# A two-layer mLSTM and retention backbone: mLSTM parts in another order, norm products at fixed positions in the last step of a stage, first two units of a stage by segment

## The chip, the cores and the metric

The kernel runs on one core of one Trainium2 chip. The metric is the device time of one execution in microseconds; what is compared is the median over runs. Engines are named as in the profile: PE is TensorE (matmuls), PEld its weight loads, DVE is VectorE, ACT ScalarE, POOL GpSimd, SP SyncE.

## The reference, cut to what matters

512 tokens of 1024 channels go through two layers. 256 of them are context tokens (segment 0), 256 latent ones (segment 1). Each layer is a half SwiGLU feed-forward, a token mixer and another half feed-forward; each of these six stages begins with an RMSNorm with a per-segment shift and scale. The mixer of the first layer is a bidirectional mLSTM, that of the second a retention.

```
def rmsnorm(h, g):
    y = hf * lax.rsqrt(jnp.mean(hf * hf, axis=-1, keepdims=True) + NORM_EPS)
def modnorm(h, g, mod, j):
    return rmsnorm(h, g) * (1 + mod[:, :, 3 * j + 1]) + mod[:, :, 3 * j]
def half_ffn(h, mod, g, w13, w2, j):
    return h + FFN_RES * mod[:, :, 3 * j + 2] * swiglu(modnorm(h, g, mod, j), w13, w2)

# one chunk of 128 tokens of the mLSTM, for one direction
s = jnp.einsum("bhtd,bhsd->bhts", q, k) * jnp.exp(d - m_t[..., None])
num = w_inter[..., None] * jnp.einsum("bhtd,bhde->bhte", q, C) + jnp.einsum("bhts,bhse->bhte", s, v)
den = w_inter * jnp.einsum("bhtd,bhd->bht", q, n) + jnp.sum(s, axis=-1)
h = num / jnp.maximum(jnp.abs(den), jnp.exp(-m_t))[..., None]
C = w_prev[..., None, None] * C + jnp.einsum("bhs,bhsd,bhse->bhde", w_s, k, v)
```

## The kernel before, in words

The residual stream XT, and the normed input as a high and a low half (xh, xl), lie channel-major in SBUF. Every weight arrives by DMA from SP as raw, and is split into wh (ACT, L148) and wl (DVE, L149). Every product is three matmuls, mm3 at L152 to L154: high by high, low by high, high by low. PSUM has four A banks and four Y banks. The six stages run in the order f00, mlstm, f01, f10, retention, f11; each is a list of units, and most units bring one weight slice of 256 columns. The matmul's moving side is 512 tokens wide, or 256 where a segment is handled by itself. Where the code has no in_order() block, a scheduler sets each engine's order from a model of the times, with the order of the code as its priority; within in_order() PE's order is that of the code.

A norm goes so. As soon as a channel tile of XT is final, ACT squares it (L170) and POOL adds the squares up into nacc (L174); the tiles 0, 6 and 7 keep theirs apart. L179 sums over channels with PE. L159 (DVE) and L161 (POOL) make rsa and rsb, the reciprocal root. L186 spreads it over the partitions with PE. Then DVE and ACT apply it tile by tile, L196 to L203: even tiles take three instructions, t, xh and xl; odd tiles go through split2 (L148, L149). In the last step of a stage (fn1 of the feed-forward, and of wout in mlstm) the products of segment 0 come first, then those of segment 1 (L414 and L594), so that segment 0's norm runs beside them; segment 1's norm comes after, beside the first products of the next stage.

mlstm at 8 heads: qk(0) to qk(3) make the queries and keys, each followed by a convolution on DVE; vo(0) and vo(1) the values of the two halves of heads, vo(2) and vo(3) the output gates; gates makes the decays, from which come nwd (in DRAM), em, ws and wp. For half hh: ktok transposes the keys (L710), states makes the chunk states C (L732), intra(s, hh) the outputs of segment s, fin(s, hh) the head norm, the gating and the transposes; wout(hh, u) projects half hh onto 512 of the output channels.

intra is the tightest part. L754 makes the scores, in two A banks. For each direction d a tile b4 (two buffers) is read from nwd by a DMA of POOL (L762), masked on POOL (L769), run through eight exps on ACT (L772) and multiplied with the scores on DVE (L775, twice). For each chunk c PE multiplies it with the values (L786) and adds the queries by C (L791), into two A banks; ACT and DVE make dn (L795 to L797), and hs from it (L801 on ACT for d = 0, L803 on DVE for d = 1). The scores hold their banks until L775 of the second direction. fin takes statistics (L817, L818), the reciprocal root as above, nb (L821), scales (DVE L824, ACT L827), gates on POOL (L832) and transposes with PE (L835) into xh and xl.

Of the kernel before, what the change touches and what calls it, by code (L numbers as in the profile page):

```python
# [23 lines left out]
KT = 8  # L24
# [64 lines left out]
def build(nc, tc, dr, out):  # L89
# [42 lines left out]
    sv = ExitStack()  # L132
# [69 lines left out]
                S.activation(out=h, in_=t, func=AF.Identity, bias=b_)  # L202
                V.scalar_tensor_tensor(out=lo, in0=t, scalar=b_, in1=h.bitcast(F32), op0=ALU.add, op1=ALU.subtract)  # L203

    def norm_seg(N, s, l, j):
        ps = bankA() if s == 0 else bankY()
        norm_apply(s, l, j, norm_bcast(norm_rstd(N, s, ps), ps))

    def accum(k, ps, gate, s):

# [65 lines left out]
    def ffn(l, which, segs, groups, on_tile, on_seg, first="seg"):  # L276
# [27 lines left out]
        for d0, nd in parts:  # L304
            for p in range(d0, d0 + nd, 2):
                sv = {}
                for ab in range(2):
                    col = ab * DFF + p * 128
                    src = w13[:, col:col + 256].rearrange("(k p) c -> p k c", p=128)

                    def half(W, hf, p=p, ab=ab, sv=sv):
                        if hf == 0:
                            sv["ps", ab] = {m: bankY() if first == "k" and p == 2 and ab == 0 else bankA() for m in range(2)}
                        ps = sv["ps", ab]
                        cols = [(a, z)]
                        if p == 0 and first == "seg" and len(segs) > 1:
                            cols = [(s * 256, s * 256 + 256) for s in segs]
                        for b, e in cols:
                            for h in (range(2) if len(cols) > 1 else (hf,)):
                                ks = range(h * 4, h * 4 + 4)  # L320
                                order = [(k, m) for k in ks for m in range(2)] if p == 0 else [
                                    (k, m) for m in range(2) for k in ks]
                                for k, m in order:
                                    mm3(ps[m][:, b:e], [W(i, k)[:, m * 128:(m + 1) * 128] for i in range(2)],
                                        (xh[:, k, b:e], xl[:, k, b:e]), k == 0, k == KT - 1)
                                if h == 0 and e == z:
                                    W.mid()

                    def done(p=p, ab=ab, sv=sv):
                        ps = sv["ps", ab]  # L330
                        for m in range(2):
                            if ab == 0:
                                sv[m] = P["s"].tile([128, 512], F32, name="s", tag="s")
                                S.activation(out=sv[m][:, a:z], in_=ps[m][:, a:z], func=AF.Silu)
                            else:
                                g = P["s"].tile([128, 512], F32, name="s", tag="s")
                                V.tensor_tensor(out=g[:, a:z], in0=sv[m][:, a:z], in1=ps[m][:, a:z], op=ALU.mult)  # L337
                                gh = P["g"].tile([128, 512], F32R, name="gh", tag="gh")
                                gl = P["g"].tile([128, 512], F32R, name="gl", tag="gl")
                                split2(g[:, a:z], gh[:, a:z], gl[:, a:z])  # L340
                                gs[p + m] = (gh, gl)

                    def fn(W, half=half, done=done, by_seg=p == 0 and first == "seg" and len(segs) > 1):
                        half(W, 0)
                        if not by_seg:
                            half(W, 1)
                        done()

                    if first == "k" and p == 0:
                        def fn0(W, ab=ab, sv=sv):  # L350
                            sv["ps", ab] = U["ps", ab] = {m: bankA() for m in range(2)}
                            first_products[ab](W)
                        res.append((fn0, src, "own"))
                        late.append((lambda W, done=done: done(), None, None))
                        if ab:
                            res += [(start, None, None)] + late
                    else:
                        res.append((fn, src, "kn" if p == 0 and first == "seg" else "k" + narrow))
            ku = [(k, min(4, d0 + nd - k)) for k in range(d0, d0 + nd, 4)]
            fin = d0 == parts[-1][0]  # L360
            for mg in range(2):
                Y = {}
                for k0, nk in ku:
# [6 lines left out]
                    last = k0 == ku[-1][0]  # L370
                    stop = last or (pair and k0 == ku[-3][0])

                    def products(W, Y, b, e, k0, nk, first, stop, done, Wm=None):
                        for h0 in range(0, nk, 2):
                            for m in range(4):
                                for k in range(h0, h0 + 2):
                                    i = mm3(Y[m][:, b:e], [W(i, k)[:, m * 128:(m + 1) * 128] for i in range(2)],
                                            [x[:, b:e] for x in gs[k0 + k]], first and k == 0, stop and k == nk - 1)
                                if stop and h0 + 2 == nk:
                                    done(m)  # L380
                            if h0 == 0 and Wm:
                                Wm.mid()
                        return i
# [19 lines left out]
                    def fn1(W, k0=k0, nk=nk, Y=Y):  # L403
# [5 lines left out]
                                on_tile(s, 4 + m)  # L409
                            return fn  # L410
                        i = products(W, Y, 0, 256, k0, nk, False, True, done(0))
                        on_seg(0)
                        Y.update({m: bankY() for m in range(4)})
                        with tc.issue_after(i.ins):  # L414
                            products(W0, Y, 256, 512, k00, nk0, True, False, None)
                            W.mid()
                            products(W, Y, 256, 512, k0, nk, False, True, done(1))
                        on_seg(1)
# [45 lines left out]
    def mlstm(on_tile, on_seg):  # L464
# [29 lines left out]
        def qk(u):  # L494
            src = win[:, u * 256:(u + 1) * 256].rearrange("(k p) c -> p k c", p=128)

            def fn(W):
                pp = {m: bankA() for m in range(2)}
                for b, e in ([(0, 256), (256, 512)] if u == 0 else [(0, 512)]):
                    for hf in range(2):  # L500
                        ks = range(hf * 4, hf * 4 + 4)
                        for k, m in ([(k, m) for k in ks for m in range(2)] if u == 0 else
                                     [(k, m) for m in range(2) for k in ks]):
                            mm3(pp[m][:, b:e], [W(i, k)[:, m * 128:(m + 1) * 128] for i in range(2)],
                                (xh[:, k, b:e], xl[:, k, b:e]), k == 0, k == KT - 1)
                        if hf == 0 and e == 512:
                            W.mid()
                for m in range(2):
                    c = u * 2 + m
                    pad = t2k(n=520).rearrange("p (s t) -> p s t", s=2)  # L510
# [7 lines left out]
                        V.scalar_tensor_tensor(out=cs, in0=pad[:, :, w:w + 256], scalar=CW[:, w * 8 + c:w * 8 + c + 1],  # L518
                                               in1=cs, op0=ALU.mult, op1=ALU.add)
                    S.activation(out=X["q" if c < 4 else "k"][c % 4 // 2][:, c % 2, :], in_=cv, func=AF.Silu)  # L520
            return (fn, src, "kn" if u == 0 else "k")

        def vo(u):
            Y = {}
# [34 lines left out]
        def wout(hh, u):  # L559
            src = dr["m_out"][hh * 512:(hh + 1) * 512, u * 512:(u + 1) * 512].rearrange("(k p) c -> p k c", p=128)  # L560

            def products(W, Y, u, b, e, done, Wm=None):
                for h0 in (0, 2):
                    for m in range(4):
                        for k in (h0, h0 + 1):
                            kk = hh * 4 + k
                            i = mm3(Y[m][:, b:e], [W(i, k)[:, m * 128:(m + 1) * 128] for i in range(2)],
                                    [z[:, kk, b:e] for z in ((xh, xl) if hh else X["y"])], k == 0, k == 3)
                        if h0:
                            done(u, m, Y[m])  # L570
                    if h0 == 0 and Wm:
                        Wm.mid()
                return i
# [16 lines left out]
            def fn1(W):  # L590
                W0 = X["W"]
                i = products(W, {m: bankA() for m in range(4)}, 1, 0, 256, done((0,)))
                on_seg(0)
                with tc.issue_after(i.ins):  # L594
                    products(W0, {m: bankY() for m in range(4)}, 0, 256, 512, done((1,)))
                    W.mid()
                    products(W, {m: bankY() for m in range(4)}, 1, 256, 512, done((1,)))
                on_seg(1)
# [2 lines left out]
        def part(f, *a):  # L601
            return (lambda W: f(X, *a), None, None)

        res += [qk(0), part(gates), qk(2)] + vo(0) + [qk(1), qk(3)]
        v1, v2, v3 = vo(1), vo(2), vo(3)

        res += [part(ktok, 0), part(states, 0), part(intra, 0, 0)] + v1 + [part(intra, 1, 0)]
        res += v2[:1] + [part(ktok, 1)] + v2[1:] + [part(states, 1), part(fin, 0, 0), part(fin, 1, 0)]
        res += v3[:1] + [part(intra, 0, 1)] + v3[1:] + [wout(0, 0), part(intra, 1, 1), wout(0, 1)]
        res += [part(fin, 0, 1), part(fin, 1, 1), wout(1, 0), wout(1, 1)]  # L610
        res.append((lambda W: st.close(), None, None))
        return res

# [625 lines left out]
                nc.sync.dma_start(out=out[t * 128:(t + 1) * 128, h * 512:(h + 1) * 512], in_=o[h])  # L1239

    def into(N, l, j):
        return (lambda s, k: norm_tile(N, s, k)), (lambda s: norm_seg(N, s, l, j))

    both = (0, 1)
    f00 = ffn(0, 0, both, [(0, range(4, 6)), (0, range(6, 10)), (0, range(10, 16))], *into(N1, 0, 1), first="k")
# [86 lines left out]
```

## Time and profile before

| | us |
|---|---|
| median of three runs (lowest, highest) | 1880.07 (1878.45, 1880.35) |
| the profiled execution: its time | 1882.0 |
| its span, first to last instruction | 1880.0 |
| PE busy | 1841.9 (98%) |
| DVE, ACT, POOL busy | 1189.4, 697.1, 166.6 |
| mean granted clock of PE | 0.992 |

A busy PE is one in which a matmul is under way; as matmuls overlap, the spacing of their starts tells more than their durations. Two ends are read from a wait: where it stood, and what its first matmul no longer overlaps with. PEclk is the granted clock of a stretch: 1.00 is the 2.4 GHz level, 0.50 the 1.2 GHz one.

### The profile page before, as it was taken

The numbers are of one execution on the slowest core, as the hardware profiler recorded it, in microseconds if no ns is written. First come the engines' busy times: TensorE is split into PE (matmuls) and PEld (weight loads), VectorE is DVE, ScalarE is ACT, GpSimd is POOL, SyncE is SP. The second block draws the span as 40 slices with busy tenths as digits, with TensorE's granted clock in tenths as the row PEclk, the third lists the DMA queues.
The fourth block names the chain that finished last, engine by engine and source line by source line (L and its number), as shares of the span: only waits on it lengthen the run. The fifth ranks groups of instructions, "written<-read, shape, count | busy, mean of one in ns | idle before, by whom it ended". The sixth has DMA issues, their size and how long they took to land.

```text
span 1880.0 us, 25438 instructions
## 1 busy us (share of the span) xinstructions
PE 1841.9 (98%) x10142; PEld 1594.1 (85%) x10142; DVE 1189.4 (63%) x1966; ACT 697.1 (37%) x1061; POOL 166.6 (9%) x204
## 2 busy tenths in 40 slices
PE   8999999999999799999999999999999999999998
PEld 6888888887788788888889888888898888889998
DVE  6858877565968566777755655555466555575554
ACT  4432233243564443223233432232254444444443
POOL 2000000110233200000001000000112120110001
PEclk9999999999999899999999999999999999989999
DMA  8545655322433234555552335545324244335652
GB/s 317 184 141 197 207 189 191 110 92 76 128 106 125 101 113 135 167 193 177 177 182 90 124 123 185 207 157 181 110 101 140 95 135 135 103 122 177 205 180 90
DMA packets 171832, 280.58 MB, mean 149 GB/s; under 512 B 6353, under 2 KB 108881, under 8 KB 171329
## 3 DMA queue, kind: packets, MB, share of 16 engines
q1 hardware_dynamic: 168800, 268.59, 42.3%
q0 software_dynamic: 2912, 10.36, 1.8%
q8 instruction: 80, 1.31, 0.3%
q14 instruction: 38, 0.31, 0.0%
q10 hardware_dynamic: 2, 0.01, 0.0%
HBM read 277.82 MB, written 1.11 MB: 148 GB/s over the span
## 4 chain that ended last, share of the span: by engine, by line
PE 90%; DVE 5%; ACT 2%; issue 1%; POOL 0%; DMA 0%; SPq 0%; POOLq 0%; DVEq 0%; ACTq 0%
PE A L153 18%; PE A L154 18%; PE A L152 18%; PE Y L153 11%; PE Y L152 11%; PE Y L154 11%; DVE wl L149 1%; PE A L786 1%; ACT wh L148 1%; PE Y L1094 1%; DVE XT L211 0%; PE Y L179 0%; DVE t L201 0%; DVE mj L1098 0%; ACT x L1109 0%
## 5 line engine op out<-in xcount | busy, mean ns | idle before, releaser
L149 DVE TENSOR_TENSOR wl<-raw,wh 128x1024 fp32r<-128x1024 f32 x360 | 448.7, 1247 | 465.4 <-ACT wh L148 465.1
L148 ACT ACTIVATE wh<-raw 128x1024 fp32r<-128x1024 f32 x360 | 382.9, 1064 | 784.1 <-PE A L153 321.8
L153 PE MATMUL A<-xl,wh 128*128 128x512 f32 (+1 forms) x1712 | 598.1, 351 | 7.0 <-DVE xl L149 6.2
L152 PE MATMUL A<-xh,wh 128*128 128x512 f32 (+1 forms) x1712 | 592.1, 352 | 4.6 <-ACT xh L1111 2.6
L154 PE MATMUL A<-xh,wl 128*128 128x512 f32 (+1 forms) x1712 | 596.6, 350 | 0.0
L153 PEld LDWEIGHTS A<-xl,wh 128*128 128x128 f32 x1712 | 324.1, 189 | 51.4 <-DVE xl L149 7.3
L152 PEld LDWEIGHTS A<-xh,wh 128*128 128x128 f32 x1712 | 320.3, 190 | 47.7 <-ACT xh L1111 2.9
L154 PEld LDWEIGHTS A<-xh,wl 128*128 128x128 f32 x1712 | 324.1, 189 | 42.2
L248 DVE CUSTOM_DVE_ANT_0 mj<-mr,mc,VB 128x1024 bf16<-128x1024 f32 x224 | 287.0, 1281 | 3.9 <-DMA mr<-mod_t 1.1
L154 PE MATMUL Y<-gh,wl 128*128 128x512 f32 (+1 forms) x704 | 244.2, 347 | 0.0
L153 PE MATMUL Y<-gl,wh 128*128 128x512 f32 (+1 forms) x704 | 244.0, 347 | 0.0
L152 PE MATMUL Y<-gh,wh 128*128 128x512 f32 (+1 forms) x704 | 243.6, 347 | 0.0
L154 PEld LDWEIGHTS Y<-gh,wl 128*128 128x128 f32 x704 | 132.2, 188 | 16.8
L153 PEld LDWEIGHTS Y<-gl,wh 128*128 128x128 f32 x704 | 132.1, 188 | 16.7
L152 PEld LDWEIGHTS Y<-gh,wh 128*128 128x128 f32 x704 | 132.0, 188 | 16.8
L153 PE MATMUL Y<-wl,xh 128*128 128x512 f32 x320 | 126.1, 394 | 0.0
L154 PE MATMUL Y<-wh,xl 128*128 128x512 f32 x320 | 125.6, 393 | 0.0
L152 PE MATMUL Y<-wh,xh 128*128 128x512 f32 x320 | 125.5, 394 | 0.0
L174 POOL TENSOR_TENSOR nacc<-nacc,nsq 128x256 f32<-128x256 f32 x50 | 41.3, 836 | 643.9 <-ACT nsq L170 642.8
L148 ACT ACTIVATE gh<-s 128x512 fp32r<-128x512 f32 (+1 forms) x88 | 48.9, 570 | 84.0 <-DVE s L337 83.9
L211 DVE SCALAR_TENSOR_TENSOR XT<-Y,GT,XT 128x256 f32<-128x256 f32 x148 | 63.7, 479 | 18.7 <-PE Y L154 18.5
L337 DVE TENSOR_TENSOR s<-s,A 128x512 f32<-128x512 f32 (+1 forms) x88 | 54.3, 619 | 27.7 <-PE A L154 26.2
(272 smaller groups left out, 1771.2 us busy)
## 6 DMA issues: line engine op xcount, KB each, us to landing
raw<-w SPq DMA_DIRECT2D x126, 1024.0 KB, 5.0
mr<-mod_t SPq DMA_DIRECT2D x128, 512.0 KB, 3.8
raw<-r_in SPq DMA_DIRECT2D x24, 1024.0 KB, 5.0
raw<-m_in SPq DMA_DIRECT2D x12, 1024.0 KB, 5.1
raw<-r_out SPq DMA_DIRECT2D x8, 1024.0 KB, 6.1
raw<-w SPq DMA_DIRECT2D x12, 512.0 KB, 3.7
w<-mod_t SPq DMA_DIRECT2D x8, 512.0 KB, 9.7
w<-mod_s SPq DMA_DIRECT2D x8, 512.0 KB, 10.1
```

The lines of the kernel that those rows point to most:

```text
L148: S.activation(out=hi, in_=src, func=AF.Copy)
L149: return V.tensor_tensor(out=lo, in0=src, in1=hi.bitcast(F32), op=ALU.subtract)
L152: TE.matmul(ps, l[0], r[0], start=first, stop=False)
L153: TE.matmul(ps, l[0], r[1], start=False, stop=False)
L154: return TE.matmul(ps, l[1], r[0], start=False, stop=last)
L174: G.tensor_tensor(out=N[s][0], in0=N[s][0], in1=sq, op=ALU.add)
L211: V.scalar_tensor_tensor(out=XT[:, k, seg(s)], in0=ps, scalar=gate[:, s, k:k + 1], in1=XT[:, k, seg(s)], op0=ALU.mult, op1=ALU.add)
L248: V.tensor_tensor_reduce(out=mp["j"], in0=raw[i], in1=mp["c"][:, w], scale=1.0, scalar=MB[:, l * 72 + f:l * 72 + f + 1], op0=ALU.mult, op1 ...
L337: V.tensor_tensor(out=g[:, a:z], in0=sv[m][:, a:z], in1=ps[m][:, a:z], op=ALU.mult)
L786: TE.matmul(pb[g][:, i, :], E[:, i * 4 + g * 2 + c], v[:, s * 2 + c, 2 * i + g, :], start=(i == 0 or n == 0), stop=(n == 0))
L1094: TE.matmul(ps, U["w", k][:, 0, c * 128:(c + 1) * 128], SC.rearrange("p (w k) -> p k w", w=2)[:, c], start=(c == 0), stop=(c == KT - 1))
```

## The change

Three things are changed.

The norm of segment 0 in the last step of f00, mlstm, f01 and f10: norm_seg with steps gives back two pieces of work, and the loop over segment 1's products calls the first (sums) ahead of its fifth product and the second (broadcast and application) ahead of its tenth. A product is three matmuls. The loop is now in_order().

The first two units of mlstm (qk(0), qk(2)) and of f01 and f10 (their first two slices) do segment 0 of both, then segment 1 of both; qk(2) had done 512 tokens at once.

The list of mlstm's parts has another order.

```
-        norm_apply(s, l, j, norm_bcast(norm_rstd(N, s, ps), ps))
+        def sums():
+            r.append(norm_rstd(N, s, ps))
+        def rest():
+            norm_apply(s, l, j, norm_bcast(r[0], ps))
+        if steps:
+            return {4: sums, 9: rest}
...
                 i = products(W, {m: bankA() for m in range(4)}, 1, 0, 256, done((0,)))
-                on_seg(0)
-                with tc.issue_after(i.ins):
-                    products(W0, {m: bankY() for m in range(4)}, 0, 256, 512, done((1,)))
+                norm = on_seg(0, True)
+                with tc.issue_after(i.ins), in_order():
+                    products(W0, {m: bankY() for m in range(4)}, 0, 256, 512, done((1,)), among=norm)
...
+                if u == 0:
+                    X["first"] = W, pp
+                    products(W, pp, 0, 256, True)
+                elif u == 2:
+                    W0, pp0 = X["first"]
+                    products(W, pp, 0, 256, False)
+                    products(W0, pp0, 256, 512, False)
+                    W.mid()
+                    conv(0, pp0)
+                    products(W, pp, 256, 512, False)
+                    conv(2, pp)
...
-        res += [qk(0), part(gates), qk(2)] + vo(0) + [qk(1), qk(3)]
+        res += [qk(0), qk(2), part(gates)] + vo(0) + [qk(1), qk(3)]
...
-        res += [part(ktok, 0), part(states, 0), part(intra, 0, 0)] + v1 + [part(intra, 1, 0)]
-        res += v2[:1] + [part(ktok, 1)] + v2[1:] + [part(states, 1), part(fin, 0, 0), part(fin, 1, 0)]
-        res += v3[:1] + [part(intra, 0, 1)] + v3[1:] + [wout(0, 0), part(intra, 1, 1), wout(0, 1)]
-        res += [part(fin, 0, 1), part(fin, 1, 1), wout(1, 0), wout(1, 1)]
+        res += [part(ktok, 0), part(states, 0), part(intra, 0, 0)] + v2[:1] + [part(intra, 1, 0)] + v2[1:]
+        res += [part(fin, 0, 0), part(fin, 1, 0), part(ktok, 1)] + v1 + [part(states, 1), part(intra, 0, 1)]
+        res += v3[:1] + [part(intra, 1, 1)] + v3[1:] + [part(fin, 0, 1), wout(0, 0), part(fin, 1, 1), wout(0, 1)]
+        res += [wout(1, 0), wout(1, 1)]
```

Line numbers behind L179 shift in the changed kernel: L754, L786, L791 and L835 of before are L801, L833, L838 and L882 after.

The end of mlstm on PE, before: the last direction of intra(1,1) (L786, L791) and the transposes of fin (L835). The products Y<-yh,wh are those of wout(0,1), the products A<-xh,wh those of wout(1,0).

```order
L154 MATMUL Y<-yh,wl 128x512
L786 MATMUL A<-v_3922,b_4928 128x129 x4
L791 MATMUL A<-C_4391,t 128x129 x4
L786 MATMUL A<-v_3922,b_4928 128x129 x4
L791 MATMUL A<-C_4367,t 128x129 x4
L152 MATMUL Y<-yh,wh 128x512
L153 MATMUL Y<-yl,wh 128x512
L154 MATMUL Y<-yh,wl 128x512
L835 MATMUL A<-ident,hs 128x128 x16
L152 MATMUL A<-xh,wh 128x256
```

Of the products of wout(0,1), 15 stand ahead of this direction and 3 behind it.

The same place on PE, after: from the scores of intra(1,1) (L801) to wout(1,0).

```order
L801 MATMUL A<-qk_3048 128x128 x8
L833 MATMUL A<-v_4368,b_4774 128x129 x4
L838 MATMUL A<-C_4504,t 128x129 x4
L833 MATMUL A<-v_4368,b_4774 128x129 x4
L838 MATMUL A<-C_4528,t 128x129 x4
L833 MATMUL A<-v_4368,b_4843 128x129 x4
L838 MATMUL A<-C_4540,t 128x129 x4
L833 MATMUL A<-v_4368,b_4843 128x129 x4
L838 MATMUL A<-C_4516,t 128x129 x4
L882 MATMUL A<-ident,hs 128x128 x16
L152 MATMUL A<-xh,wh 128x256
```

All products of wout(0,0) and wout(0,1) now stand ahead of these rows, and both directions follow the scores directly.

The last step of f00 on PE, before: where the broadcast of segment 0's norm stands. The sums (L179) come after 26 matmuls of segment 1, this after 60 in all.

```order
L152 MATMUL Y<-gh,wh 128x256
L153 MATMUL Y<-gl,wh 128x256
L154 MATMUL Y<-gh,wl 128x256
L186 MATMUL A<-ident,rsb 128x128 x2
L152 MATMUL Y<-gh,wh 128x256
L153 MATMUL Y<-gl,wh 128x256
```

The same step after: the sums, with the first twelve matmuls of segment 1 ahead of them.

```order
L153 MATMUL Y<-gl,wh 128x256
L154 MATMUL Y<-gh,wl 128x256
L179 MATMUL A<-ones,nacc 128x1 x6
L152 MATMUL Y<-gh,wh 128x256
L153 MATMUL Y<-gl,wh 128x256
```

The broadcast follows 15 matmuls behind the sums.

## Rows read from the trace of the kernel before

**Rows 1.** The page: busy us of each engine (share of the span), instructions.

```profile
PE 1841.9 (98%) x10142; PEld 1594.1 (85%) x10142; DVE 1189.4 (63%) x1966; ACT 697.1 (37%) x1061; POOL 166.6 (9%) x204
```

**Rows 2.** Waits of PE over the span: total us, times, longest us.

```profile
PE A L835 <- POOL hs L832: 9.4, 1, 9.4
PE A L153 <- DVE xl L149: 6.2, 6, 1.7
```

**Rows 3.** Border f00 to mlstm: timeline (start, us, what, [idle before]); window (us, PE busy, ...).

```profile
396.33 1.39 PE L179 MATMUL A<-ones,nacc 128*128 128x1 f32 x12
398.65 0.72 POOL L161 TENSOR_TENSOR rsb<-rsa,mhalf 128x2 f32<-128x2 f32 x1 [4.66 <-DVE rsa L159]
401.68 0.60 PE L186 MATMUL A<-ident,rsb 128*128 128x128 f32 x4
409.13 0.39 PE L153 MATMUL A<-xl,wh 128*128 128x256 f32 x1 [1.66 <-DVE xl L149]
414.54 0.60 PE L186 MATMUL Y<-ident,rsb 128*128 128x128 f32 x4
...
406.00:431.00 25.00, 21.79 (x148) 1.00 0.35 110
```

**Rows 4.** End of mlstm: timeline of PE; windows (us, PE busy, PEclk, DMA share, GB/s).

```profile
617.31 0.72 PE L791 MATMUL A<-C,t 64*128 64x129 f32 x8
629.24 2.34 PE L835 MATMUL A<-ident,hs 128*128 128x128 f32 x8 [9.45 <-POOL hs L832]
631.23 0.56 PE L152 MATMUL A<-xh,wh 128*128 128x256 f32 x1
...
618.00:631.30 13.30, 3.74 (x22) 0.73 0.23 79
624.00:634.40 10.40, 5.05 (x23) 0.51 0.46 157
631.60:634.30 2.70, 2.70 (x14) 0.50 0.85 329
```

**Rows 5.** Windows of 256-column, 512-column, and 512-column weight-moving products.

```profile
386.05:392.05 6.00, 6.00 (x53) 1.00 0.54 175
209.00:256.00 47.00, 47.00 (x209) 1.00 0.53 173
424.00:431.00 7.00, 7.00 (x32) 1.00 0.39 117
```

**Rows 6.** Longest wait of PE at the borders after mlstm, f01 and f10: timeline.

```profile
659.98 0.39 PE L153 MATMUL A<-xl,wh 128*128 128x256 f32 x1 [0.63 <-DVE xl L149]
1025.98 0.39 PE L153 MATMUL A<-xl,wh 128*128 128x256 f32 x1 [1.56 <-DVE xl L149]
1391.69 0.39 PE L153 MATMUL A<-xl,wh 128*128 128x256 f32 x1 [1.59 <-DVE xl L149]
```

**Rows 7.** Weights of intra(0,0): the second eight exps, and their first use: timeline.

```profile
483.55 2.46 ACT L772 ACTIVATE b<-b,a 128x128 f32<-128x128 f32 x8
514.26 0.61 PE L786 MATMUL A<-v,b 128*128 128x129 f32 x4
```

**Rows 8.** Weights of intra(1,1), and the freeing of a bank: timeline; median landing, us.

```profile
590.42 0.58 POOL L762 DMA_DIRECT2D b<-nwd  x1 [1.99 <-PE A L786]
596.27 1.69 POOL L769 TENSOR_SCALAR_AFFINE_SELECT b<-b 128x1024 f32<-128x1024 f32 x1 [5.26 <-DMA b<-nwd]
597.99 2.47 ACT L772 ACTIVATE b<-b,a 128x128 f32<-128x128 f32 x8 [2.87 <-POOL b L769]
602.81 2.49 DVE L775 SCALAR_TENSOR_TENSOR b<-A,b 128x512 f32<-128x512 f32 x4
610.00 1.15 ACT L801 ACTIVATE hs<-A,dn 128x128 f32<-128x128 f32 x4 [0.37 <-DVE dn L797]
...
b<-nwd POOLq DMA_DIRECT2D x8, 512.0 KB, 4.7
```

## What the change will do to the time: the prediction

> **What bounds the kernel now.** I read the page's summary first: PE is busy for 1841.9 of 1880.0 us [rows 1]. So nearly every microsecond that a change can give lies in stretches where PE stands still or runs at the lower clock. The waits of PE say where these are. The longest single wait is 9.4 us, L835 (the transposes of the last mLSTM heads) for the gated heads of L832; then come six waits of 6.2 us in all, the longest 1.7, for the low half xl (the odd tiles, L149) [rows 2]. The six are boundaries between stages: the first products of the next stage wait until the RMSNorm of a segment has been summed (L179), rooted (L159, L161), broadcast (L186) and applied.
>
> Two stretches were then read instruction by instruction. At the border f00 to mLSTM [rows 3] the sums of segment 0 start at 396.33, 26 matmuls after the first segment-1 product, rsb follows on GpSimd at 398.65, and the broadcast stands on PE only at 401.68. PE runs out of work at 407.5 and idles 1.66 us for xl. Segment 1 follows with four shorter waits. Of 25.00 us between 406 and 431, 21.79 are busy, so 3.2 are idle [rows 3]. A first matmul after a wait also loses its overlap: it is 0.39 us long where its successors come every 0.118, so I count 5 x 0.27 = 1.4 more: 4.6 us lost at this border.
>
> At the end of mLSTM [rows 4] the last intra matmuls (L791) end at 618.0. Then dn, the last hs on DVE, the head norm's statistics, its reciprocal root on GpSimd, scaling and gating lie one behind the other; the transposes resume at 629.24 after 9.45 us of idle, and wout(1,0) starts at 631.23. From 624.00 to 634.40 the granted clock is 0.51, that is, the 1.2 GHz level, and the products of wout(1,0) come every 0.21 us in it (2.70 us for 12 to 13) rather than every 0.118: some 15 of them, about 1.5 us, and a further 1.2 on the transposes. The tail costs about 9.5 + 2.7 = 12 us.
>
> **The change part by part.** The arithmetic is the same. Only qk(2) has more matmuls: 96 of 256 columns for 48 of 512. At 6.00/51 = 0.118 us and 47.00/207 = 0.227 us [rows 5] (two of each window's count were under way at its start), that is 11.3 for 10.9, or **+0.4 us**.
>
> *Norms at fixed positions, first two units by segment.* At f00 to mLSTM the sums come after 12 matmuls rather than 26 and the broadcast 15 matmuls (1.8 us) later; the last squares that they need may come some tenths after PE gets there. The chain of segment 0 then starts at about 394.7, 1.6 us sooner, and its broadcast, which had stood 5.4 us behind the sums, stands about 3 behind: it comes some 4 us sooner. That covers the 1.66. After the broadcast of segment 1, 16 matmuls of segment 0 are left (1.9 us); from L186 at 414.54 PE goes on until its waits at about 416 to 418, so that 0.7 to 1.2 us remain. **Gain 3.5 us.** On the three later borders the longest idle was 0.63, 1.56 and 1.59 us [rows 6]. In the new order 9 products follow the second broadcast at f01 (1.1 us, about what is lost there now: no gain), 21 at f10 (2.5 us, which covers most: gain 1.5), and at retention the broadcast stands only 4 matmuls behind the sums, so PE may wait there for rsa and rsb: gain 1.7, give back 0.5. **Sum of the later borders: 2.7, bounds 0.5 to 4.**
>
> *The order of the mLSTM parts.* The gates are computed 11 us later, since the 96 products of qk(2) now stand ahead of them; from their results come the exps of intra(0,0)'s weights, the second set of which ACT ends at 486.0, for a first use by PE at 514.26 [rows 7]; 11 us later they still arrive in time, and the cover is vo(0), qk(1) and qk(3). The products of wout(0,0) and wout(0,1), 96 matmuls, are what fills the tail today: the order of before has 43 + 29 + 1 + 15 + 3 of them between intra(0,1) and the last transposes. In the new one fin(0,0) and fin(1,0) come sooner, so these products are free sooner, and the order spends all 96 between the states of the second half and the end of intra(0,1): 4 are left ahead of the scores of intra(1,1), and from there to wout(1,0) there is none, as the quoted rows show.
>
> So PE meets the tail with nothing to do, and the tail becomes a chain of latencies. From the first mLSTM product at 406.4 to there the new order has 596 matmuls of 512 columns (0.227 or, with the weight as the moving side, 7.00/30 = 0.233 us apart [rows 5]: 136.5 in all), 192 of 256 (22.7) and some 200 small ones, 37 us by the starts of their like in the trace (0.18 on average): 196. With 2 us of remaining stalls PE ends intra(0,1) at about 604.5. That frees the second weight buffer (b4 has two). From there [rows 8] give: issue 0.5 on GpSimd; from issue to landing 4.7, the median of the eight, though one took 5.8 (590.42 to 596.27); the select 1.4 (this one 1.69); eight exps 2.5; two products on DVE at 0.62 each and half a microsecond of what stands between them, 1.7: 604.5 + 0.5 + 4.7 + 1.4 + 2.5 + 1.7 = 615.3. Only then can the second chunk of direction 0 run, because the banks that it needs hold the scores which direction 1 reads. Second chunk of direction 0, first of direction 1, bank freed through dn and hs (1.8: hs alone is 1.15 on ACT), second chunk: 1.8 + 1.8 + 1.8, so 620.7 (a pair of L786 and L791 groups is 1.8 by the pair that ends at 618.03). From the last L791 to the resumed transposes are 11.2 us today (618.0 to 629.24) and to wout(1,0) 13.2: **634.0 for 631.23, a loss of 2.8 us**, in which the 3.5 of the first border and the 0.4 of qk(2) are contained. With 5.8 us of landing it is 635.1, with as much less 632.9, and if the first buffer is late too, 636.
>
> *The clock in it.* In the present tail PE is busy for 3.74 of 13.30 us, at a mean granted clock of 0.73 [rows 4]. In the new one it has about 9 us of work in the 30 from 604.5 to 634, the same share, so I take the same 0.73 for the small matmuls there: 9/0.73 is 3.3 more, of which about half stand on the chain just added up (the first scores and the first chunk run while something else is waited for). I take **1.5**, bounds 0 and 3.3. The recovery in wout(1,0) costs what it costs now.
>
> The Trainium skill (page "DMA: Bandwidth & Descriptors", section "Anatomy of one DMA") has a GpSimd-issued copy at about 2 us fixed plus bytes over 436 GB/s, 3.2 us for these 512 KB: an estimate by that page that would bring the tail 1.5 us forward and the time to about 1880. The trace has 4.7 as its median, 1.5 more than that fit, and the sum goes by the trace.
>
> **Sum.** 1882.0 (the profiled execution, 1880.0 span and 2.0 around it) + 2.8 + 1.5 - 2.7 = 1883.6. The median of the runs is 1.9 below the profiled execution, so about 1881.7; I say **1882**. That lies within 0.2% of 1880.07 (3.8 us, about what a measurement of this kernel can tell from no change).
>
> **Rivals.** (a) *The tail is covered after all.* If the first wait of 9.4 goes because the heads of fin(0,1) and fin(1,1) end while PE still has products, the 9.5 and the 2.7 of clock are saved, with 3.5 at the border, 0.4 of qk(2) against and 2.7 later: 1880 - 18 = 1862. Even half of the wait gives 1870. For it speaks that both fin parts stand earlier in the text; against it, that no filler is left in the row of PE. It decides itself by whether the new chain ends before 629. (b) *Slower, by the weight buffers.* If both copies of the b4 tiles of intra(1,1) take the longer landing, and the small matmuls all run at the 1.2 GHz level, the tail ends at 636, the clock costs 3.3 on the intra matmuls and another 1.5 on wout(1,0), if as many of its products again run at 0.21: +4.8 + 4.8 - 2.7 = +6.9, 1887; with the later borders giving only 0.5, 1889. The point from which it decides is a wout(1,0) that starts later than about 636. (c) *The fixed positions wait themselves.* With PE's order fixed, a sums product whose squares are late, or a broadcast 15 matmuls (1.8 us) behind the sums whereas rsb ends 1.65 us behind them today (397.72 to 399.37) and rsa can stand behind the split of a weight on DVE, stops PE at each of four borders for 0.5 to 1.5 us: the borders give nothing and the time is 1884 to 1886.
>
> **How the numbers follow.** The forecast, between 1876.3 and 1883.8, gets 0.42. (a), whole or in part, gets 0.25: the reading of the order is firm, but the chain has ten steps, and two microseconds less in it with the borders at their best is enough for 1876. (b) and (c) get 0.33 together. The range reaches to half of (a), 1869, and to the end of (b) with a little over, 1890.
>
> **What would show it.** Right: the idle ahead of the transposes is split into several waits from about 605 to 633, wout(1,0) starts at 632.5 to 636 on the present time line, the 1.66 at the first border is gone, and the 1.56 and 1.59 too. The 1.2 GHz level would hold for longer than the present 10.4 us. Wrong: a tail in which wout(1,0) starts before 629, wout(0,1) products still running on PE when the last intra ends, or new waits of L186 for rsb at the borders that eat the gain.

## The result and the profile after

The changed kernel takes 1891.97 us (median of 4 runs, 1888.17 to 1894.37) where before takes 1880.06; the ratio is 1.0063, 95% interval 1.005 to 1.0075. It is slower by 0.63%, and 2 us above the upper end of the forecast range.

The page and the waits of PE of the changed kernel (total us, times, longest us):

```profile
PE 1848.2 (98%) x10190; PEld 1602.7 (85%) x10190; DVE 1188.6 (63%) x1966; ACT 698.3 (37%) x1063; POOL 168.3 (9%) x204
PE A L882 <- POOL hs L879: 10.7, 3, 8.4
PE A L833 <- DVE hs L850: 4.7, 1, 4.7
...
PE A L152 <- ACT xh L202: 2.2, 2, 1.1
PE A L801 <- DVE hs L850: 2.0, 1, 2.0
PE Y L186 <- POOL rsb L161: 1.6, 2, 1.0
PE A L179 <- POOL nacc L174: 1.4, 1, 1.4
PE A L833 <- ACT hs L848: 1.2, 1, 1.2
```

Against [rows 2], the six waits for xl have left the list. In their place stand waits inside intra (L801, L833), two more ahead of the transposes, and one of the sums L179 for nacc. Windows of the changed kernel (us, PE busy, PEclk, DMA share, GB/s), the border f00 to mlstm first, then the stretches at the 1.2 GHz level that matter:

```profile
406.00:431.00 25.00, 25.00 (x207) 1.00 0.25 69
611.00:622.00 11.00, 5.39 (x36) 0.69 0.41 139
631.90:642.10 10.20, 4.45 (x20) 0.50 0.21 72
655.80:662.60 6.80, 6.80 (x33) 0.50 0.01 4
1410.00:1413.60 3.60, 3.60 (x19) 0.53 0.00 0
```

The border that idled for 3.2 us [rows 3] is busy throughout: all its idle is gone. Where the time went is told by the same landmarks in each trace. Executions differ by up to 2 us in when f00 ends, so I measure between landmarks (line numbers shift by a few in the runs): S0, S1, S2 and S3 are the first product of segment 1 in the last step of f00, mlstm, f01 and f10; W is the start of wout(1,0); G is the one pair of gates products that spreads the maxima over the partitions (L677, after: L724), nearly the last thing that gates asks of PE; I is the first weighted product of intra(0,0) (L786, after: L833); R is the first sums product of the norm behind retention. In the changed kernel's timeline of PE (start, us, what, [idle before]) S0, G, I, the waits in the tail and W are:

```profile
391.52 0.28 PE L152 MATMUL Y<-gh,wh 128*128 128x256 f32 x1
477.76 0.48 PE L724 MATMUL A<-rows,ones 1*128 1x128 f32 x2
524.21 0.68 PE L833 MATMUL A<-v,b 128*128 128x129 f32 x4
611.84 0.90 PE L801 MATMUL A<-qk 64*128 64x128 f32 x4 [1.99 <-DVE hs L850]
618.20 1.20 PE L833 MATMUL A<-v,b 128*128 128x129 f32 x4 [4.71 <-DVE hs L850]
626.22 1.01 PE L833 MATMUL A<-v,b 128*128 128x129 f32 x6 [1.20 <-ACT hs L848]
637.54 0.69 PE L882 MATMUL A<-ident,hs 128*128 128x128 f32 x2 [8.36 <-POOL hs L879]
639.53 0.56 PE L152 MATMUL A<-xh,wh 128*128 128x256 f32 x1
```

and in that of before S0 and G, beside W and I of [rows 4, 7]:

```profile
393.27 0.28 PE L152 MATMUL Y<-gh,wh 128*128 128x256 f32 x1
468.85 0.48 PE L677 MATMUL A<-rows,ones 1*128 1x128 f32 x2
```

The same differences for every kernel of this study, in us (S0 to G is 477.76 less 391.52 in the changed one, and so on). Each row is one profiled execution, the medians are of all; kernels with the same order of PE differ by up to 1.6 us in a stretch (G to I is 46.7 in f4, 45.1 in h1), so a difference below that in one row can be one of executions:

| kernel | S0-G | G-I | I-W | S0-W | W-S1 | S1-S2 | S2-S3 | S3-R | median us |
|---|---|---|---|---|---|---|---|---|---|
| before | 75.6 | 45.4 | 117.0 | 238.0 | 12.8 | 365.7 | 366.2 | 298.0 | 1880.1 |
| changed | 86.2 | 46.4 | 115.3 | 248.0 | 12.6 | 369.8 | 364.3 | 299.4 | 1892.0 |
| e1_norm | 75.2 | 45.4 | 116.8 | 237.3 | 13.2 | 365.1 | 364.3 | 299.3 | 1879.8 |
| e2_first_two | 84.0 | 44.6 | 116.9 | 245.5 | 12.6 | 365.9 | 366.2 | 298.8 | 1888.5 |
| e3_parts | 75.6 | 45.4 | 116.3 | 237.3 | 13.4 | 365.7 | 366.2 | 298.6 | 1878.9 |
| e4_no_parts | 86.2 | 45.5 | 110.9 | 242.7 | 12.1 | 370.4 | 364.3 | 299.4 | 1886.8 |
| f1_gates_late | 83.6 | 45.9 | 112.3 | 241.8 | 12.1 | 365.7 | 366.2 | 298.8 | 1884.7 |
| f2_gates_early | 73.7 | 45.2 | 114.6 | 233.4 | 13.3 | 369.1 | 364.3 | 300.2 | 1881.4 |
| f3_no_step_mlstm | 86.2 | 46.2 | 115.6 | 248.0 | 13.4 | 365.9 | 364.3 | 300.2 | 1889.1 |
| f4_gates_early_two | 73.7 | 46.7 | 114.1 | 234.6 | 12.5 | 366.8 | 364.3 | 298.6 | 1876.8 |
| g6_hold | 86.2 | 46.2 | 113.3 | 245.7 | 12.0 | 369.9 | 364.3 | 299.6 | 1891.2 |
| g4_short_weights | 86.2 | 41.9 | 110.1 | 238.3 | 12.7 | 368.2 | 364.3 | 298.8 | 1875.9 |
| g5_f4_old_list | 73.7 | 46.6 | 117.7 | 238.0 | 13.3 | 365.7 | 364.3 | 298.1 | 1878.6 |
| h1_gate_dve | 73.7 | 45.1 | 113.3 | 232.1 | 12.4 | 365.6 | 364.3 | 298.2 | 1874.0 |

So the changed kernel loses 10.0 us from S0 to W and 4.1 from S1 to S2, gains 1.9 from S2 to S3, and loses 1.4 from S3 to R; behind R it gains 0.8. The loss up to W is about as large as the delay of the gates, 10.6.

### The profile page after: what moved, and what is told of

It reads as the page before. It is cut to its first block, busy times and chain, and to the rows that moved or that the text cites. A ratio compares the mean times of both kernels' runs of the same rounds, so it can differ in the third digit from the quotient of the medians.

```text
span 1890.9 us, 25521 instructions
## 1 busy us (share of the span) xinstructions
PE 1848.2 (98%) x10190; PEld 1602.7 (85%) x10190; DVE 1188.6 (63%) x1966; ACT 698.3 (37%) x1063; POOL 168.3 (9%) x204
## 3 DMA queue, kind: packets, MB, share of 16 engines
HBM read 277.82 MB, written 1.11 MB: 148 GB/s over the span
## 4 chain that ended last, share of the span: by engine, by line
PE 91%; DVE 2%; ACT 2%; DMA 1%; issue 1%; POOL 1%; POOLq 0%; DVEq 0%; SPq 0%; ACTq 0%
PE A L153 18%; PE A L152 18%; PE A L154 18%; PE Y L152 11%; PE Y L153 11%; PE Y L154 11%; PE Y L1141 1%; PE A L833 1%; ACT b L819 0%; DMA mc<-cc 0%; ACT wh L148 0%; DMA t<-nwd 0%; PE Y L179 0%; PE A L179 0%; POOL nacc L174 0%
## 5 line engine op out<-in xcount | busy, mean ns | idle before, releaser
L341 ACT ACTIVATE s<-A 128x512 f32<-128x512 f32 (+1 forms) x86 | 46.1, 536 | 69.7 <-PE A L154 69.7
```

## The experiments

Ratios are to the kernel before on the same chip, with 95% intervals. The first four take the change apart.

**e1_norm**: the fixed norm positions alone.

```
-                on_seg(0)
-                with tc.issue_after(i.ins):
+                norm = on_seg(0, True)
+                with tc.issue_after(i.ins), in_order():
...
```

> Before with only the fixed positions of segment 0's norm products in the last step of f00, mlstm, f01 and f10; qk(2) and the list of mlstm's parts are as before, and the tail of mlstm on PE has the same 43, 29, 1, 15 and 3 filler products. Theory (the loss of the changed kernel is the tail of mlstm, which has no filler products left): the tail stays as before, wout(1,0) starts at 631 less what the first border gives, so the time is 1876 to 1882. Rival (the fixed positions themselves cost the time, by waits for nacc and rsb and by the half clock behind them): at least two borders get longer by 2 us each, 1883 to 1888.

Measured: 1879.76 us, ratio 0.9998 (0.9989 to 1.0008). No border gets 2 us longer. f01 to f10 gains 1.9, f10 to retention loses 1.3, and the border f00 to mlstm gives S0 to W only 0.7: with one unit's products of segment 0 alone, PE waits there for the second broadcast (0.48) and for xh (1.11) instead, and the granted clock is 0.50 from 416.2 to 419.6, right behind these waits.

**e2_first_two**: the first two units by segment alone, with gates behind qk(2).

```
-        res += [qk(0), part(gates), qk(2)] + vo(0) + [qk(1), qk(3)]
+        res += [qk(0), qk(2), part(gates)] + vo(0) + [qk(1), qk(3)]
...
+                elif u == 2:
+                    products(W, pp, 0, 256, False)
+                    products(W0, pp0, 256, 512, False)
```

> Before with only the first two units of mlstm, f01 and f10 by segment (and gates behind qk(2)); norm products and list of parts as before. PE's order has 26, 7, 13, 35 and 14 filler products in and behind intra(0,1), the last 14 ahead of the first direction of intra(1,1) and none behind it. Theory (filler): the tail is between the two kernels, a total wait of PE of 10 to 14 us from the scores of intra(1,1) on; the first border loses 2 us rather than 4.6; the time is 1879 to 1885. Rival (only the new list costs): the tail is as before and the time 1876 to 1880.

Measured: 1888.5 us, 1.0043 (1.0028 to 1.0058), above what either theory gave. This part alone carries 7.5 of the 10.0 us up to W.

**e3_parts**: the new list from ktok(0) on, alone (the three lines of the list in the diff).

> Before with only the new list of mlstm's parts from ktok(0) on; norm products and qk as before. PE's order still has 28 filler products between the scores of intra(1,1) and its first weights, and 15 ahead of the second direction. Theory (filler, not the list): the time is that of before within 3 us, 1877 to 1883, and the wait ahead of the last transposes stays 8 to 10 us, with no wait over 2 us at the scores or at the first weights of intra(1,1). Rival (the list itself, by the later gate units, values and states, costs the 8 us): wout(1,0) starts at 636 to 640 and the time is 1886 to 1891.

Measured: 1878.88 us, 0.9991 (0.9981 to 1.0). The new list by itself costs nothing, and keeps its fillers. What uses them up in the changed kernel is not the list alone: e2, with the old list, has 14 ahead of the first direction and none behind.

**e4_no_parts**: the changed kernel with the old list.

> The changed kernel with the old list of mlstm's parts from ktok(0) on: fixed norm positions and first two units by segment stay. PE's order has 22 filler products between the scores of intra(1,1) and its weights and 7 ahead of the second direction. Theory (filler): the first border's 4.6 us are gained, the tail costs 0 to 2 us more than before's, f01 to f10 gains 1.8, f10 to retention loses 3: 1876 to 1881. Rival (fixed positions or the half clock behind them cost most): 1884 to 1890 as in the changed kernel.

Measured: 1886.78 us, 1.0038 (1.0023 to 1.0053): between the two. With the old list the changed kernel still loses 4.7 up to W. Both theories fall in part: the old list gives back about half, the rest stays. What e2 and e4 share, and e1 and e3 lack, is S0 to G longer by 8.4 to 10.6 us. The next two try that; f3 and f4 take up the later borders.

**f1_gates_late**: before, with gates moved and nothing else.

```
-        res += [qk(0), part(gates), qk(2)] + vo(0) + [qk(1), qk(3)]
+        res += [qk(0), qk(2), part(gates)] + vo(0) + [qk(1), qk(3)]
```

> Before with one edit: gates stands behind qk(2) instead of ahead of it; qk(2) is still 48 products of 512 columns, the list and the norm products are as before. Theory (the gates start the chain that ends mlstm; whatever delays them delays wout(1,0), and PE spends its fillers while it waits): gates' last products come 9 to 11 us later, first intra products 6 to 9 us later, wout(1,0) starts at 636 to 640 for 631.2, and the time is 1885 to 1890. Rival (in the kernels with the first two units by segment it is the split of qk(2) and the later convolution of qk(0) that cost, not the gates): wout(1,0) stays within 2 us of 631 and the time is 1878 to 1882.

Measured: 1884.74 us, 1.0023 (1.0012 to 1.0033). One moved part costs 0.23%. G comes 8.0 later and W 3.8: less than I expected, since I to W is 4.7 us shorter than before, but clear of the rival; the time lies just under the expected 1885. PE's idle time from S0 to W is only 0.8 us longer than before, 14.8 for 14.1. The rest goes with the clock: PE works at 0.50 for 3.4 us from 508.7 and 3.4 from 617.9, beside 1.9 us ahead of W that before has as well; at half speed that costs, as an estimate, 3.4 us. Why e2, with the same place of the gates, takes 3.8 us more than f1 is not shown. S0, G, I and W:

```profile
391.59 0.28 PE L152 MATMUL Y<-gh,wh 128*128 128x256 f32 x1
475.17 0.48 PE L677 MATMUL A<-rows,ones 1*128 1x128 f32 x2
521.06 0.61 PE L786 MATMUL A<-v,b 128*128 128x129 f32 x4
633.40 0.56 PE L152 MATMUL A<-xh,wh 128*128 128x256 f32 x1
```

**f2_gates_early**: the changed kernel, with gates ahead of segment 1 of qk(2).

```
                     conv(0, pp0)
+                    gates(X)
                     products(W, pp, 256, 512, False)
...
-        res += [qk(0), qk(2), part(gates)] + vo(0) + [qk(1), qk(3)]
+        res += [qk(0), qk(2)] + vo(0) + [qk(1), qk(3)]
```

> The changed kernel with one edit: gates is called inside the second unit, behind segment 1 of qk(0) and its convolution, ahead of segment 1 of qk(2). All else of the change stays. PE's order now has 28 filler products between the scores of intra(1,1) and its first weights and 15 ahead of the second direction. Theory (gates): the gates come within 2 us of before's time, wout(1,0) starts at 629 to 632, the first border's gain shows, the late borders as in the changed kernel (mlstm to f01 up to 4 longer, f10 to retention 1 to 3 longer): 1876 to 1884. Rival (the split first units or the new list cost it): wout(1,0) stays at 636 to 640 and the time at 1888 to 1893.

Measured: 1881.42 us, 1.0007 (0.9999 to 1.0016). Half a unit of order gives back 10.6 us of the 11.9. G is 12.5 sooner than in the changed kernel, W 14.6, and W is sooner than the expected 629 to 632:

```profile
393.22 0.28 PE L152 MATMUL Y<-gh,wh 128*128 128x256 f32 x1
466.89 0.48 PE L725 MATMUL A<-rows,ones 1*128 1x128 f32 x2 [1.24 <-DVE rows L720]
512.04 0.61 PE L834 MATMUL A<-v,b 128*128 128x129 f32 x4
626.63 0.56 PE L152 MATMUL A<-xh,wh 128*128 128x256 f32 x1
```

**f3_no_step_mlstm**: the changed kernel without fixed positions in mlstm's last step.

```
-        if steps:
+        if steps and (l, j) in ((0, 1), (1, 0), (1, 1)):
...
-                with tc.issue_after(i.ins), in_order():
+                with tc.issue_after(i.ins), (in_order() if norm else ExitStack()):
```

> The changed kernel without the fixed positions in the last step of mlstm alone (sums and broadcast of f01's first norm are left to the scheduler, as before). The tail stays at its 8 us loss. Theory (the sums at the fifth product wait 1.4 to 3 us for nacc, whose squares stand behind mc on ACT, and the second stretch at half clock, 655.8 to 662.6, follows from that wait): no wait at these sums, no second half-clock stretch, the stretch from wout(1,0) to f01's norm 3 to 4 us shorter than in the changed kernel: 1886 to 1890. Rival (the second half-clock stretch comes from the tail itself): the clock still falls at about 655 and the time stays within 1 us of 1891.

Measured: 1889.12 us, 1.0046 (1.0033 to 1.0059). S1 to S2 falls from 369.8 to 365.9, the wait of the sums is gone, and the clock stays high where it had fallen (window of this run):

```profile
655.80:668.00 12.20, 12.11 (x102) 1.00 0.30 88
```

The wait itself, in the changed kernel: ACT works on mc (L309), whose DMA is issued by POOL behind the last gating, and the last squares of segment 0 stand behind that on ACT.

```profile
648.58 2.01 ACT L309 ACTIVATE mc<-mc 128x1024 f32<-128x1024 f32 x2
653.72 0.70 ACT L170 ACTIVATE nacc<-XT 128x256 f32<-128x256 f32 x2
655.02 2.03 PE L179 MATMUL A<-ones,nacc 128*128 128x1 f32 x12 [1.35 <-POOL nacc L174]
```

So a position that was free at f00 is not free at mlstm. In e1 the same sums waited for nothing.

**f4_gates_early_two**: early gates, and fixed positions in f00 and f01 alone.

```
-        if steps:
+        if steps and (l, j) in ((0, 1), (1, 0)):
...
                     conv(0, pp0)
+                    gates(X)
...
-        res += [qk(0), qk(2), part(gates)] + vo(0) + [qk(1), qk(3)]
+        res += [qk(0), qk(2)] + vo(0) + [qk(1), qk(3)]
```

> The changed kernel with gates inside the second unit as in the run with early gates, and fixed norm positions in f00 and f01 alone (mlstm and f10 leave theirs to the scheduler). Theory: all that gains is left, the first border (4 us) and f01 to f10 (1.8 us), and all that loses is gone: 1873 to 1877. Rival (the gain at the first border is eaten by the tail, which is a chain from the gates and not PE's work): 1877 to 1880.

Measured: 1876.84 us, 0.9979 (0.9969 to 0.9988): faster than both kernels.

**g5_f4_old_list**: that kernel with the old list.

> The kernel with early gates and fixed norm positions in f00 and f01 alone, with the old list of mlstm's parts. PE's order has before's fillers in the tail again: 43, 29, 1, 15 and 3. Theory (with the gates on time the list is worth nothing by itself): wout(1,0) within 1.5 us of that kernel, and 1875 to 1879. Rival (the new list brings some of the gain): slower by 3 us or more, 1879 to 1883.

Measured: 1878.59 us, 0.9999 (0.999 to 1.0008). S0 to W is 238.0, what it was before, though the border's idle is gone and the gates come 1.9 us sooner. Most of the gain goes ahead of I: two new waits at the gates' own matmuls (1.25 and 0.83) and 3.2 us of work at a clock of 0.50, from 466.6. The rest goes from I to W, 117.7 for 117.0. W comes 3.4 us earlier with the new list (234.6), more than the theory's 1.5, while the time of 1878.6 lies in the theory's range, not in the rival's. The two intervals just miss each other (0.9988 and 0.999). So the new list is likely worth something once the gates are early; by how much is open.

**g6_hold**: the changed kernel with wout(0,1) held behind intra(1,1)'s scores, so that the tail has its fillers again.

```
+                with (tc.issue_after(X["sc"].ins) if u else ExitStack()):
+                    products(W, {m: bankY() for m in range(4)}, u, 0, 512, done((0, 1)), W)
...
+                        X["sc"] = TE.matmul(sb[g][:, x:x + 128], k[o:o + 64, i, ti[c]], q[o:o + 64, i, ti[c]],
```

> The changed kernel with one edit: wout(0,1)'s 48 products may not be issued before the last score product of intra(1,1). All else stays, late gates included. PE's order then has 32 products behind the scores, 15 ahead of the second direction and 1 ahead of the transposes; between the scores and the end of intra(0,1) only 3 are left of 51. Theory (PE's order: products put ahead of intra(0,1) hold up the release of the weight buffers, and leave nothing for the tail): intra(0,1) runs 6 to 10 us sooner, wout(1,0) starts 5 to 9 us sooner than the changed kernel's 639.5, the time is 1881 to 1886. Rival (the stretch from the gates to wout(1,0) is a chain of latencies of about 160 us whatever PE does meanwhile): wout(1,0) stays within 2 us and the time is 1889 to 1893.

Measured: 1891.19 us, 1.0066 (1.005 to 1.0081): no faster than the changed kernel. 48 products now stand between the scores and the transposes, the last L838 ends 4.2 us sooner, and yet W comes only 2.3 us sooner, as the wait ahead of the last transposes grows. The time fits the rival, W lies just outside its 2 us. What this run does not change is how much is left behind I: 230 products of 512 columns, as in the changed kernel.

```profile
623.15 0.72 PE L839 MATMUL A<-C,t 64*128 64x129 f32 x8
...
635.07 2.34 PE L883 MATMUL A<-ident,hs 128*128 128x128 f32 x8 [9.90 <-POOL hs L880]
637.06 0.56 PE L152 MATMUL A<-xh,wh 128*128 128x256 f32 x1
```

**g4_short_weights**: the changed kernel with the weights' preparation cut short (no mask, one pass for the exps).

```
-            G.affine_select(out=E, in_=E, pattern=[[0, 8], [sg, 128]], base=0, channel_multiplier=-sg,
-                            compare_op=ALU.is_ge, fill=NEG)
-            for x in range(8):
-                S.activation(out=E[:, x], in_=E[:, x], func=AF.Exp, bias=X["a"][:, r0 + x:r0 + x + 1])
+            S.activation(out=E, in_=E, func=AF.Identity, bias=X["a"][:, r0:r0 + 1])
```

> The changed kernel with the preparation of intra's weights cut short: the mask on GpSimd (1.1 to 1.9 us a tile) is left out, and the eight exps (2.45 us) are one pass without exp (about 1.1 us), so the output is not the reference's. Theory (the two weight tiles of intra(1,1) are links of the tail): each of the two links is 2.5 to 3 us shorter, wout(1,0) starts 5 to 8 us sooner than 639.5, and the time is 1883 to 1887. Rival (the tail waits for DVE and the head norm, not for the weights): wout(1,0) within 2 us of 639.5, and 1889 to 1893.

Measured in one execution, so without an interval: 1875.9 us; W comes 9.7 us sooner than in the changed kernel, more than I expected, and with the late gates still in it. 4.5 of them lie between G and I, where 16 exps on ACT are two passes, 5.2 behind I. The scheduler put other products into the tail as well (11 ahead of the scores), so the sizes of the parts are not clean; that the weights are links of the chain is.

**h1_gate_dve**: the kernel of f4 with the last two gating products on DVE.

```
-            G.tensor_tensor(out=hf, in0=hf, in1=X["so"][hh][:, t, :], op=ALU.mult)
+            (V if s and hh else G).tensor_tensor(out=hf, in0=hf, in1=X["so"][hh][:, t, :], op=ALU.mult)
```

> The kernel with early gates and fixed norm positions in f00 and f01 alone, with one edit: the two gating products of fin(1,1), the last ones of mlstm, are done by DVE instead of GpSimd, where they took 2.49 us. PE's order is the same row for row. Theory (the end of mlstm is a chain of latencies in which these two are links): DVE does them in about 1.2 us, the wait ahead of the last transposes falls from 8.4 to 7.4 to 7.8 us, wout(1,0) starts 0.8 to 1.5 us sooner, and the time is 1874 to 1876.5 for 1876.8. Rival (something else ends there at the same time): the wait stays above 8 us and the time at 1876 to 1879.

Measured: 1873.96 us, 0.997 (0.9959 to 0.998), the lowest median of the study, 18 us below the changed kernel. The wait and W, first in f4, then here:

```profile
624.85 1.11 PE L884 MATMUL A<-ident,hs 128*128 128x128 f32 x4 [8.37 <-POOL hs L881]
626.85 0.56 PE L152 MATMUL A<-xh,wh 128*128 128x256 f32 x1
```

```profile
622.79 1.34 DVE L881 TENSOR_TENSOR hs<-hs,so 128x512 f32<-128x512 f32 x2
623.62 1.73 PE L884 MATMUL A<-ident,hs 128*128 128x128 f32 x7 [7.90 <-DVE hs L881]
625.21 0.56 PE L152 MATMUL A<-xh,wh 128*128 128x256 f32 x1
```

PE's order is the same in both. The wait is 0.5 shorter (7.9, just above the range), and I to W 0.8, as expected of two links that got shorter; the other 1.6 that S0 to W is shorter lie ahead of I, where the kernels are alike: in f4 the granted clock is 0.50 from 468.8 to 472.2 with PE busy throughout, in h1 it is 1.00 there. The time lies just under the expected range. That this kernel beats before is measured; that it beats f4 is not, as the two intervals overlap.

## Why the prediction was wrong, step by step

**The gates: the step that failed.** The prediction saw that the gates come 11 us later (10.6 measured) and priced it at nothing, because the exps of intra(0,0) end at 486.0 for a use at 514.26 [rows 7], 28 us of slack. That slack is still there in the changed kernel: the exps end at 497.3, 27 us ahead of I. But I itself has moved. In all kernels but g4 the first intra product follows G by 44.6 to 46.7 us, whether G is early or late, and W follows I by 111 to 118. (In f1 and e4, with late gates and the old list, it is 111 to 112, so some of the delay is absorbed there; in e2, with the same two, it is 116.9.) One tile that is ready early says that this tile is not the last link; it doesn't say that what stands behind the gates has time. The windows S0 to I, I to W and G to I show what the delay did (us, PE busy, matmuls, PEclk, DMA share, GB/s), before and changed:

```profile
393.27:514.26 120.99, 117.62 (x670) 1.00 0.32 100
514.26:631.23 116.97, 106.28 (x657) 0.97 0.31 102
468.85:514.26 45.41, 45.25 (x244) 1.00 0.44 140
391.52:524.21 132.69, 131.37 (x783) 1.00 0.33 101
524.21:639.53 115.32, 96.37 (x590) 0.92 0.27 92
477.76:524.21 46.45, 45.13 (x244) 1.00 0.41 121
```

From G to I PE hardly waits, 0.2 us before and 1.3 in the changed kernel, and holds 244 matmuls in both; DVE is busy there for 41.5 and 37.8 us. So these 45 us are a distance in the order that the scheduler gave PE; whether the chip could start I sooner behind late gates was not tried (with fewer exps it was 41.9, g4). Late gates put more of PE's work ahead of I and leave less behind it, 230 products of 512 columns for 295, about 15 us at 0.227. Yet I to W is only 1.7 us shorter: that stretch is not set by PE's work. PE is idle in it for 19.0 us instead of 10.7, and works for 8.8 us at the 1.2 GHz level instead of 1.9. From S0 to W that is 6.2 us more of idle and, as an estimate at half speed, 3.5 us for the clock, of 10.0. Shown is that gates alone cost 0.23% when moved (f1), and that putting them forward gives back 10.6 of 11.9 us (f2).

**The first border.** Of the idle, 0.7 to 1.2 us were to remain; all 3.2 are gone. But the gain was put into the sum as if it reached W. In g5 the idle is gone too and W is no sooner: new waits at the gates, a stretch at half clock and a slightly longer way from I to W take it back.

**The tail.** The mechanism was right, and so was its length: from the end of PE's work on intra(0,1) to W the sum gave 604.5 to 634.0, 29.5 us, and 1.5 for the clock; the trace has 608.91 to 639.53, 30.6. The weight tiles (timeline of POOL and ACT, changed kernel) went as worked out, with ACT's exps ahead of dn of the direction before:

```profile
606.95 1.10 POOL L816 TENSOR_SCALAR_AFFINE_SELECT b<-b 128x1024 f32<-128x1024 f32 x1 [4.10 <-DMA b<-nwd]
609.46 0.58 POOL L809 DMA_DIRECT2D b<-nwd  x1 [1.41 <-PE A L833]
613.57 1.91 POOL L816 TENSOR_SCALAR_AFFINE_SELECT b<-b 128x1024 f32<-128x1024 f32 x1 [3.53 <-DMA b<-nwd]
608.08 2.45 ACT L819 ACTIVATE b<-b,a 128x128 f32<-128x128 f32 x8 [2.25 <-POOL b L816]
610.44 0.20 ACT L842 ACTIVATE dn<-A 128x2 f32<-128x2 f32 x2
```

The copy that was issued at 609.46 had landed by 613.57, 4.1 us. The Trainium skill's fit for such a copy (page "DMA: Bandwidth & Descriptors", section "Anatomy of one DMA"), an estimate of 3.2 us, is short of it here too. What was mis-sized is the start, for which the sum had 2 us of stalls: it came 6.2 us later than worked out (608.91 less 391.52 against 604.5 less 393.27). What of it I can name are waits for states and head norms at 509, 511, 572 and 573 us, 3.5 us of idle, and 3.4 us at the lower clock behind them. And the cause that I gave, no fillers left, does not carry the loss: g6 puts 48 back behind the scores and the time moves by 0.8 us. e3 and f2, with gates on time, keep theirs under the new list, so missing fillers here are rather what late gates look like in PE's order.

**The later borders.** Forecast -2.7, bounds -0.5 to -4; measured +2.6 from W on. f01 to f10 is right (-1.9 for -1.5). At mlstm to f01 "no gain" became +4.1: rival (c), in its words "a sums product whose squares are late", took place there (wait 1.35), and behind it came what I had not priced, 6.8 us at the 1.2 GHz level. At f10 to retention the wait of L186 for rsb came as told; I had set it at 0.5 against a gain of 1.7, but with the wait for xh behind it (0.53 and 1.11) and a stretch at the lower clock it became +1.4. Together the start and these borders, 6.2 and 5.3 us, are more than the 9.0 by which the profiled execution, 1892.6, missed the sum of 1883.6; f00 ended 1.8 us sooner in it.

**The rivals.** (a) had the sign of f4 and h1, but by the gates, not by the fin parts. (b) had the sign and nearly the size, 1889, by the wrong place: W passed its mark of 636, but the weight tiles took no longer than usual (4.7 and 4.1 us to land), they began later. The range ended there, 2 us short.

## What to carry to other kernels

Where a stage ends in a long wait of the busiest engine, see whether its length follows that engine's work. Here I to W did not, with 230 products in it or 295; moving fillers about behind the scores changed 0.8 us (g6), idle time removed ahead of it did not reach its end (g5), and moving the part that it starts from did (f2). To judge a part that is moved back, measure what follows it at a fixed distance, over more than one trace if there is one, rather than the slack of one buffer; and ask whether that distance is waiting or only the order of the work. A norm's place in PE's order that is free in one stage has to be checked in each stage against what its squares stand behind.

## What was not expected of the hardware

A short wait was followed by a long stretch at the lower clock while PE was busy. In the changed kernel the sums waited 1.35 us at 655.02, after a tail with little work, and from 655.80 to 662.60 the granted clock was 0.50 with PE busy for 6.80 of 6.80 us. Without that wait (f3) it was 1.00 there. At 1410 us waits of 0.53 and 1.11 us were followed by 3.4 us at half clock with PE busy throughout, while in the kernel before the wait of 1.59 us at the same border [rows 6] was followed by none. Nor does the wait alone decide it: f2, f4, g5 and h1 have the same order of PE around G and the same waits there (1.24 to 1.25 and 0.83 us), and the clock fell to 0.50 for 3.4 us behind them in f4 and g5, and stayed at 1.00 in f2 and h1. What made the difference no run here shows.
